# The down projection of a two-layer decoder trunk by Strassen's seven products per four blocks, with whole-block weight splitting

## The chip, the cores and the metric

The kernel runs on one core of one Trainium2 chip, as one program in one launch. The metric is the device time of one execution in microseconds (us); lower is better. TensorE (PE) multiplies; VectorE (DVE), ScalarE (ACT) and GpSimd (POOL) do the elementwise work; SyncE (SP) issues the transfers. Each engine runs its own instructions in the order in which the program gives them.

## The reference

Two layers work on one prompt of 512 tokens and 8 samples of 4 new tokens, that is 544 columns of width 1024. Only the feed-forward part is touched in its arithmetic:

```python
for l in range(DEPTH):                       # DEPTH = 2
    x = x + mixer(rms_norm(x, norm1_w[l]))   # w_in, retention and dilated attention, w_out
    x = x + conv_ffn(rms_norm(x, norm2_w[l]))
y = rms_norm(x, final_norm_w)

def conv_ffn(h, ctx, w_up_l, conv_w_l, conv_b_l, w_down_l):   # D_FF = 2816, so w_up is 1024 x 5632
    u = h @ w_up_l
    ext = jnp.concatenate([ctx, u], axis=1)
    c = conv_b_l
    for j in range(CONV_W):                  # a causal depthwise convolution of width 3
        c = c + ext[:, j:j + T] * conv_w_l[j]
    g, val = c[..., :D_FF], c[..., D_FF:]
    return (silu(g) * val) @ w_down_l        # 2816 x 1024
```

## The kernel before

**Tiles.** Activations are held with the channel on the 128 partitions and the tokens along the row. The residual stream is 8 tiles `x0` to `x7` of [128, 2, 272]: 128 channels, and the 544 tokens as two halves c of 272 columns (256 prompt and 16 sample tokens). Every large product is fp32 made of three passes in a half format: with a weight `w = wh + wl` and an activation `r = rh + rl` it is `wh·rh + wh·rl + wl·rh`. One matmul is 128x128 weights against 272 columns, and a block with k input tiles has 3 x k x 2 of them, which add up in one pair of PSUM banks called `ps` (one bank for each half of the columns).

**Weights.** Of each block SP loads a part of up to 4 input tiles into `raw` (`load_w`, six such buffers), ACT copies it into `wh` and DVE subtracts, `wl = raw - wh` (`split_w`, five pairs). A block of 8 input tiles comes in two halves.

**The feed-forward part.** There are 44 up blocks (8 input tiles, 48 matmuls each), two for each of the 22 row tiles `y` of the hidden layer: the gate and the value. What a finished bank goes through is called the conv chain below. DVE makes `u = ps * rstd` (two instructions, 512 prompt and 32 sample columns), ACT makes `c` (560 columns with the borders of the convolution), two DVE instructions add the other two taps to `c`, ACT applies SiLU for the gate, DVE multiplies the two into `y` (two instructions), ACT makes `yh` and DVE `yl`. POOL fills the borders of `u` and copies the last columns of it. The 22 tiles are taken in groups, `GROUPS`: after the up blocks of group g+1 come the 8 down blocks of group g, one for each of the 8 tiles of x, with as many input tiles as the group has (5, 5, 4, 4, 4). Each ends with one DVE instruction, `x[n] += ps` over 544 columns. The down blocks of the last group of layer 0 follow those of the group before it directly, and then `w_in` of layer 1. In layer 1 the last group goes over the columns in two passes, one for each c, so that the final norm can begin.

**Order.** PE's stream is the list `main`. All other work is written as generators of pieces, and a planner (`Stream`, with a `Clock` of its own that estimates each engine's progress) puts the pieces between PE's matmuls when it thinks that their inputs are there. Names in `URGENT` may be placed on an engine with a backlog. So the order on DVE, ACT and POOL is fixed when the program is made; on the chip an engine waits at its next instruction whatever stands behind it. All instructions pass through one helper, so they all carry line L112 (L117 after the change).

Of the kernel before, what the change touches and what calls it, by code (L numbers as in the profile page):

```python
# [9 lines left out]
F32 = mybir.dt.float32  # L10
# [14 lines left out]
GROUPS = ((0, 5), (5, 10), (10, 14), (14, 18), (18, 22))  # L25
# [17 lines left out]
EARLY = 640  # L43

# [105 lines left out]
URGENT = ("evac", "norm", "tail", "ffn", "feed", "split")  # L150
# [75 lines left out]
def trunk(ctx: ExitStack, tc: tile.TileContext, xin, w_in, w_out, w_up, w_down, kc, vc, s0, sctx_d, params_d,  # L226
# [70 lines left out]
    def add_block(src, nk, rhs, evac, pre=None):  # L297
        i = len(main)
        parts = [(0, nk)] if nk <= 4 else [(0, (nk + 1) // 2), ((nk + 1) // 2, nk)]
# [3 lines left out]

    raw, split = {}, {}

    def load_w(s):
        if s < len(halves):
            i, a, b = halves[s]
            raw[s] = rotate(wpool.tile([128, b - a, 128], F32, name=name("raw"), tag="raw", bufs=6), "raw", 6)
            sp.dma_start(raw[s], main[i]["src"][:, a:b, :])  # L310

    def split_w(s, at_once=False):
        if s < len(halves):
            i, a, b = halves[s]
# [211 lines left out]

    class Layer:
# [88 lines left out]
    def att_sample(L, l, g):  # L616
        rows = [slice(32 * i, 32 * i + 32) for i in range(4)]
        for hp in range(4):
            yield pace(L)
            kt = L.kt.pop((g, hp))  # L620
            yield PE(L.qpad, L.ks, *kt, banks=0 if hp else 2)
# [3 lines left out]
            qs = [L.qpad[:, hp, 4 * g + i, :] for i in range(4)]  # L625
# [97 lines left out]
    def ret_head(L, l, h):  # L723
# [4 lines left out]
        for b in range(NB):  # L728
            pool.tensor_mul(L.qdp[:, h, b, b * T:(b + 1) * T], q[:, SEQ + b * T:SEQ + (b + 1) * T],
# [95 lines left out]
    def ret_sample(L, l):  # L825
        yield PE(*[t for h in range(4) for t in L.s0[h]], L.qdp, L.sts, L.vss, banks=1)
        po = sec([128, 128])
        for b in range(NB):
            for h in range(4):
                pe.matmul(po[32 * h:32 * h + 32, :], lhsT=L.qdp[:, h, b, :], rhs=L.s0[h][b // 4][:, b % 4, :],  # L830
                          start=b == 0, stop=False, tile_position=(0, 32 * h))
        for h in range(4):
            pe.matmul(po[32 * h:32 * h + 32, :], lhsT=L.sts[:, h, :], rhs=L.vss[:, h, :], start=False, stop=True,
                      tile_position=(0, 32 * h))
        yield EW("dve", po)
# [22 lines left out]
    def ret_state(L, l):  # L858
        units = [(h, g) for h in range(4) for g in range(2)]
        bds = []  # L860
        for i in range(len(units) + 2):
            if i < len(units):
                h, g = units[i]
                bd = work.tile([96, 4, 128], F32R, name=name("bd"), tag="bd", bufs=3)
# [3 lines left out]
            if i >= 2:  # L868
# [7 lines left out]
                dve.scalar_tensor_tensor(s, s, DECAY_S[h], ps, op0=OP.mult, op1=OP.add)  # L876
                done()
                store(sret_o[l, h, :, g * 4:g * 4 + 4, :], s)
        L.s0 = None


    def mixer(l):
# [10 lines left out]
        def begin():  # L893
            st.spawn(norm.finish(), "norm")
            rope_tables(L, l, 2)()
            L.qpad = work.tile([128, 4, NB, 32], F32, name=name("qpad"), tag="qpad", bufs=1)
            pool.memset(L.qpad, 0.0)
            L.ks = small([128, 4, 32], "ks", 1)
            L.vs = small([32, 512], "vs", 1)
# [8 lines left out]
            def samples():  # L908
# [486 lines left out]
```

## Time and profile before

| what | value |
|---|---|
| three runs | 1446.16, 1446.17, 1448.29 us; median 1446.17 us |
| the profiled execution: its time | 1444.82 us |
| its span | 1443.0 us, mean granted TensorE clock 0.997 of full speed |
| PE busy | 1423.1 us, 99% of the span |
| DVE busy | 949.2 us, 66% |
| ACT busy | 571.6 us, 40% |
| POOL busy | 178.9 us, 12% |
| chain of work that ended last | 94% PE, 3% DVE, 1% issue |

The busy shares are means over stages with different limits. The chain of work that ended last is followed back from the last instruction; its share says on which engine the end waits.

### The profile page before, as it was taken

The numbers are of one execution on the slowest core, as the hardware profiler recorded it, in microseconds if no ns is written. First come the engines' busy times: TensorE is split into PE (matmuls) and PEld (weight loads), VectorE is DVE, ScalarE is ACT, GpSimd is POOL, SyncE is SP. The second block draws the span as 40 slices with busy tenths as digits, with TensorE's granted clock in tenths as the row PEclk, the third lists the DMA queues.
The fourth block names the chain that finished last, engine by engine and source line by source line (L and its number), as shares of the span: only waits on it lengthen the run. The fifth ranks groups of instructions, "written<-read, shape, count | busy, mean of one in ns | idle before, by whom it ended". The sixth has DMA issues, their size and how long they took to land.

```text
span 1443.0 us, 29646 instructions
## 1 busy us (share of the span) xinstructions
PE 1423.1 (99%) x11634; PEld 1356.0 (94%) x11634; DVE 949.2 (66%) x1857; ACT 571.6 (40%) x1108; POOL 178.9 (12%) x553
## 2 busy tenths in 40 slices
PE   8999999999999999999999999999999999999997
PEld 8888788999999999999998878899999999999996
DVE  8876556588775565757678765566977647566665
ACT  4454333444443333424435442243444424333334
POOL 4212222000000000000022221120000000000003
PEclk9999999999999999999999999999999999999999
DMA  6315682433222222223322339722422232322231
GB/s 237 97 60 181 233 311 89 154 113 115 93 80 88 91 83 101 93 84 104 104 90 90 119 105 316 283 91 101 148 104 88 65 112 70 107 88 89 88 93 63
DMA packets 98635, 173.92 MB, mean 121 GB/s; under 512 B 11072, under 2 KB 21440, under 8 KB 98496
## 3 DMA queue, kind: packets, MB, share of 16 engines
q1 hardware_dynamic: 98496, 172.03, 35.3%
q8 instruction: 92, 1.51, 0.4%
q14 instruction: 47, 0.39, 0.1%
HBM read 159.77 MB, written 12.21 MB: 119 GB/s over the span
## 4 chain that ended last, share of the span: by engine, by line
PE 94%; DVE 3%; issue 1%; DMA 0%; ACT 0%; SPq 0%; DVEq 0%; POOL 0%; ACTq 0%
PE ps L112 82%; PE sec L112 12%; DVE wl L112 1%; DVE rb L112 1%; DMA x<-xin 0%; DVE p L112 0%; SPq L112 0%; DVE xl L112 0%; DVE ra L112 0%; DVE sq L112 0%; ACT xh L112 0%; DVE va L112 0%; POOL qa L112 0%; DVEq L1381 0%; DVE tmp L112 0%
## 5 line engine op out<-in xcount | busy, mean ns | idle before, releaser
L112 PE MATMUL ps<-xh,wh 128*128 128x272 f32 x2304 | 489.0, 294 | 1.4 <-ACT wh L112 1.1
L112 PE MATMUL ps<-xh,wl 128*128 128x272 f32 x2304 | 477.3, 289 | 0.7 <-DVE wl L112 0.7
L112 PE MATMUL ps<-xl,wh 128*128 128x272 f32 x2304 | 477.3, 289 | 0.0
L112 PEld LDWEIGHTS ps<-xh,wh 128*128 128x128 f32 x2304 | 361.2, 189 | 19.0 <-issue 14.7
L112 PEld LDWEIGHTS ps<-xh,wl 128*128 128x128 f32 x2304 | 362.3, 189 | 0.9 <-DVE wl L112 0.9
L112 PEld LDWEIGHTS ps<-xl,wh 128*128 128x128 f32 x2304 | 362.3, 189 | 0.0
L112 ACT ACTIVATE wh<-raw 128x512 fp32r<-128x512 f32 (+2 forms) x432 | 248.3, 598 | 172.0 <-PE ps L112 158.8
L112 DVE TENSOR_TENSOR wl<-raw,wh 128x512 fp32r<-128x512 f32 (+2 forms) x432 | 295.9, 703 | 18.7 <-ACT wh L112 17.9
L112 DVE SCALAR_TENSOR_TENSOR c<-u,taps,c 128x560 f32<-128x560 f32 x176 | 141.2, 802 | 89.0 <-ACT c L112 85.9
L112 ACT ACTIVATE c<-u,taps 128x560 f32<-128x560 f32 x88 | 75.5, 857 | 227.1 <-DVE u L112 223.7
L112 DVE TENSOR_TENSOR x<-x,ps 128x544 f32<-128x544 f32 (+1 forms) x120 | 81.7, 681 | 119.6 <-PE ps L112 119.2
L112 PE MATMUL ps<-yh,wh 128*128 128x272 f32 x704 | 150.9, 288 | 0.0
L112 PE MATMUL ps<-yh,wl 128*128 128x272 f32 x704 | 150.5, 288 | 0.0
L112 PE MATMUL ps<-yl,wh 128*128 128x272 f32 x704 | 150.4, 288 | 0.0
L112 DVE TENSOR_TENSOR u<-ps,rstd 128x512 f32<-128x512 f32 (+1 forms) x176 | 69.2, 435 | 80.5 <-PE ps L112 80.4
L112 PEld LDWEIGHTS ps<-yh,wh 128*128 128x128 f32 x704 | 112.3, 188 | 0.1
L112 PEld LDWEIGHTS ps<-yl,wh 128*128 128x128 f32 x704 | 112.2, 188 | 0.1
L112 PEld LDWEIGHTS ps<-yh,wl 128*128 128x128 f32 x704 | 112.3, 188 | 0.0
L112 POOL COPY last<-u 128x2 f32<-128x2 f32 (+1 forms) x176 | 28.2, 192 | 667.2 <-DVE u L112 630.3
L112 DVE TENSOR_TENSOR rb<-ps,rope 32x544 f32<-32x544 f32 (+1 forms) x96 | 69.2, 721 | 1.4
L112 ACT ACTIVATE yh<-y 128x544 fp32r<-128x544 f32 x44 | 29.0, 659 | 82.6 <-DVE y L112 82.6
L112 PE MATMUL ps<-ch,wh 128*128 128x272 f32 x256 | 53.4, 290 | 0.0
(147 smaller groups left out, 1343.3 us busy)
## 6 DMA issues: line engine op xcount, KB each, us to landing
raw<-w_up SPq DMA_DIRECT2D x176, 256.0 KB, 2.8
raw<-w_in SPq DMA_DIRECT2D x112, 256.0 KB, 3.9
kt<-kc SPq DMA_DIRECT2D x80, 256.0 KB, 5.2
vt<-vc SPq DMA_DIRECT2D x80, 256.0 KB, 5.2
raw<-w_down SPq DMA_DIRECT2D x48, 256.0 KB, 2.6
raw<-w_out SPq DMA_DIRECT2D x32, 256.0 KB, 2.7
raw<-w_down SPq DMA_DIRECT2D x32, 192.0 KB, 2.4
s<-s SPq DMA_DIRECT2D x16, 256.0 KB, 5.3
```

What stands on the lines that cost most here:

```text
L112: return f(*args, **kw)
```

## The change

The 1024 rows of the output, in 8 tiles, and the hidden tiles of a group are taken in two by two blocks: two tiles of x (`x1` for the even, `x2` for the odd one, in the code's names), two hidden tiles a and b, each with its two column halves. What took 8 block products (2 x tiles, 2 hidden tiles, 2 halves) now takes seven, in the form that keeps partial sums (Winograd's). A *unit* is one pair of x tiles over one group: with 4 hidden tiles it has 7 products of 6 matmuls, 42 in all, where the two down blocks had 48. Strassen's form serves groups 1 to 5 of layer 0 and 1 to 4 of layer 1; group 0 and the last group of layer 1 stay plain. There are 36 units. The groups become (2, 4, 4, 4, 4, 4).

- **Weights of a unit** (`split_unit`): four raw blocks per pair of hidden tiles, in a new layout `q_down` (prepared by the host). POOL makes three sums and DVE one (256 elements per partition each, tile `sums`, one buffer; one unit at a time). ACT copies 768 elements of `raw` and 1024 of `sums` to `wh`, DVE subtracts 768 and 1024 for `wl`.
- **Activations of a pair of hidden tiles** (`make_forms`): POOL makes four differences of 272 columns (`fa`, `fb`); ACT and DVE make the hi and lo parts of them (`fh`, `fl`, 544 each, two of each) and of the plain tiles (`hb`, `lb` 544; `h1`, `l1` 272). These take the place of `yh` and `yl`.
- **Products** (`Unit`): the order on PE is P1, P7, P3 of the unit before, P6, P4, P2, P5. P1, P6, P5 and P3 add up in one bank (half 1 of `ps`), P7 and P4 in another (`sec`), P2 in half 0. Between two products that share a bank the partial sum is read: after P1 ACT copies it to `one` and POOL adds that to `x1`; after P6 and after P5 ACT copies it to `snap`, and after P5 POOL (DVE in the last group of layer 0) adds the 544 columns of `snap` to `x2`; after P7 and after P4 DVE adds 272 columns to `x2`; after P3 DVE adds 544 to `x1`. P6 waits for the copy after P1, P5 for that after P6, P3 for that after P5, P4 for DVE's addition after P7.
- **Whole blocks**: `raw`, `wh`, `wl` hold 8 input tiles in three buffers each; a block is loaded three blocks ahead and split in one instruction per engine in the middle of the block two ahead. Only the first two blocks of the program keep halves.
- **Small tiles** of the mixers (`qpad`, `qdp`, `k3`, `v3`, `vs`, `vss`, `bd`) move from pools of their own to the common buffers; two are made in two halves.

```diff
-GROUPS = ((0, 5), (5, 10), (10, 14), (14, 18), (18, 22))
+GROUPS = ((0, 2), (2, 6), (6, 10), (10, 14), (14, 18), (18, 22))
+AT = {"P1": 0, "P7": 1, "P6": 3, "P4": 4, "P2": 5, "P5": 6, "P3": 9}
+WEIGHT = {"P1": 0, "P2": 1, "P4": 2, "P5": 3, "P6": 4, "P7": 5, "P3": 6}
+UNITS = 3
...
+    def split_unit(s, nk):
+        yield IF(lambda: not splitting)
+        splitting.append(s)
+        w = raw.pop(s)
+        sums = wpool.tile([128, nk, 4, 128], F32, name=name("sums"), tag="sums", bufs=1)
...
+        yield EW("pool", w)
+        pool.tensor_add(sums[:, :, 0], w[:, :, 3], w[:, :, 2])
+        pool.tensor_sub(sums[:, :, 1], sums[:, :, 0], w[:, :, 0])
+        yield EW("act", w)
+        act.activation(hi[:, :, 0:3], w[:, :, 0:3], AF.Copy)
+        dve.tensor_sub(sums[:, :, 2], w[:, :, 0], w[:, :, 3])
+        pool.tensor_sub(sums[:, :, 3], w[:, :, 1], sums[:, :, 1])
+        yield EW("dve", hi)
+        dve.tensor_sub(lo[:, :, 0:3], w[:, :, 0:3], hi[:, :, 0:3].bitcast(F32))
+        yield EW("act", sums)
+        act.activation(hi[:, :, 3:7], sums, AF.Copy)
+        yield EW("dve", hi)
+        dve.tensor_sub(lo[:, :, 3:7], sums, hi[:, :, 3:7].bitcast(F32))
+        splitting.pop()
...
+    def make_forms(a, b, first, i, dst):
+        fa, fb = blk([128, 2, HC], F32, "fa"), blk([128, 2, HC], F32, "fb")
+        pool.tensor_sub(fa[:, 0], a[:, 1], a[:, 0])
+        pool.tensor_sub(fa[:, 1], b[:, 1], fa[:, 0])
+        pool.tensor_sub(fb[:, 0], b[:, 1], a[:, 1])
+        pool.tensor_sub(fb[:, 1], b[:, 0], fa[:, 1])
...
+    class Unit:
...
+            before = {"P4": "P7", "P6": "P1", "P5": "P6", "P3": "P5"}.get(p)
+            if before:
+                st.until(lambda: before in self.seen)
...
+            if p == "P1":
+                self.one = blk([128, HC], F32, "one")
+                act.activation(self.one, bank[:, :HC], AF.Copy)
+                yield EW("pool", self.one)
+                pool.tensor_add(x1[:, 0], x1[:, 0], self.one)
+            elif p == "P7":
+                dve.tensor_add(x2[:, 1], x2[:, 1], bank[:, :HC])
+            elif p == "P6":
+                act.activation(self.snaps[:, 0], bank[:, :HC], AF.Copy)
+            elif p == "P5":
+                act.activation(self.snaps[:, 1], bank[:, :HC], AF.Copy)
+                eng = ("dve", dve) if last else ("pool", pool)
+                yield EW(eng[0], self.snaps)
+                eng[1].tensor_add(x2, x2, self.snaps)
...
-            load_w(s + 6)
-            split_w(s + 3)
+            load_w(s + 3)
...
+                if k == (a + e) // 2:
+                    split_w(s + 2)
```

Over the whole program PE issues 216 matmuls of 272 columns fewer (24 in each of the nine groups that use the form), ACT 14 instructions fewer, DVE 30 fewer, and POOL 252 more: 108 sums, 72 differences of the forms, 36 additions of `one`, 32 of `snap` (four more are DVE's) and 4 fills of halved tiles.

The order at one place shows what stands in each engine's queue: the last up blocks before a group's down projection in the middle of layer 0, and the start of that projection (before: group 2, blocks `x0`, `x1`; after: group 3, units of `x0`, `x1` and of `x2`, `x3`). On DVE, before, the conv chain of the last up block (`u`, `c`, `y`) is followed by half-block weights and the additions from `ps`:

```order
L112 TENSOR_TENSOR wl_1312_7612<-raw_1295_7498,wh_1311_7611 128x512
L112 TENSOR_TENSOR u_1313_7640<-ps_1306_7576,rstd_829_4249 128x512
L112 TENSOR_TENSOR u_1313_7640<-ps_1306_7576,rstd_829_4249 128x8x4
L112 SCALAR_TENSOR_TENSOR c_1314_7645<-u_1313_7640,taps_78,c_1314_7645 128x560 x2
L112 TENSOR_TENSOR wl_1318_7653<-raw_1298_7530,wh_1317_7652 128x512
L112 TENSOR_TENSOR x0_69<-x0_69,ps_1315_7649 128x544
L112 TENSOR_TENSOR y_1323_7695<-c_1305_7572,c_1314_7645 128x2x256
L112 TENSOR_TENSOR y_1323_7695<-c_1305_7572,c_1314_7645 128x2x16
```

After the change, the same place on DVE:

```order
L117 TENSOR_TENSOR u_1134_7333<-ps_1129_7268,rstd_748_4092 128x512
L117 TENSOR_TENSOR u_1134_7333<-ps_1129_7268,rstd_748_4092 128x8x4
L117 TENSOR_TENSOR wl_1133_7307<-sums_1131_7305,wh_1132_7306 128x2x512
L117 SCALAR_TENSOR_TENSOR c_1135_7338<-u_1134_7333,taps_78,c_1135_7338 128x560 x2
L117 TENSOR_TENSOR x1_70<-x1_70,sec_1139_7352 128x272
L117 TENSOR_TENSOR y_1141_7375<-c_1128_7264,c_1135_7338 128x2x256
L117 TENSOR_TENSOR y_1141_7375<-c_1128_7264,c_1135_7338 128x2x16
L117 TENSOR_TENSOR sums_1142_7379<-raw_1130_7269 128x2x128
```

The weight subtraction of 1024 elements for the next unit and the two `c` instructions now stand ahead of the addition after P7 (`x1_70<-x1_70,sec`), for which P4 waits. On ACT, before and after:

```order
L112 ACTIVATE c_1314_7645<-u_1313_7640,taps_78 128x560
L112 ACTIVATE wh_1317_7652<-raw_1298_7530 128x512
L112 ACTIVATE wh_1321_7686<-raw_1307_7577 128x512
L112 ACTIVATE yh_1324_7717<-y_1323_7695 128x544
```

```order
L117 ACTIVATE c_1135_7338<-u_1134_7333,taps_78 128x560
L117 ACTIVATE one_1140_7356<-ps_1137_7344 128x272
L117 ACTIVATE snap_1138_7345<-ps_1137_7344 128x272
L117 ACTIVATE wh_1143_7380<-raw_1130_7269 128x2x384
L117 ACTIVATE wh_1143_7380<-sums_1142_7379 128x2x512
L117 ACTIVATE snap_1138_7345<-ps_1137_7344 128x272
L117 ACTIVATE one_1149_7422<-ps_1146_7407 128x272
```

The copy after P1 (`one`), for which P6 waits, stands behind the last `c` of the conv chain; the second `snap` of unit 0, for which its P3 waits, and the `one` of unit 1 stand behind the copy of 1024 `sums`, which waits for POOL. On POOL, before, only border copies stand there:

```order
L112 MEMSET u_1313_7640 128x2
L112 COPY u_1313_7640<-ctx_813_4174 128x8x2
L112 COPY last_814_4176<-u_1313_7640 128x2
L112 COPY last_814_4176<-u_1313_7640 128x16
```

After the change:

```order
L117 COPY last_733_4014<-u_1134_7333 128x16
L117 TENSOR_TENSOR x0_69<-x0_69,one_1140_7356 128x272
L117 TENSOR_TENSOR sums_1142_7379<-raw_1130_7269 128x2x128
L117 TENSOR_TENSOR sums_1142_7379<-sums_1142_7379,raw_1130_7269 128x2x128
L117 TENSOR_TENSOR sums_1142_7379<-raw_1130_7269,sums_1142_7379 128x2x128
L117 TENSOR_TENSOR x1_70<-x1_70,snap_1138_7345 128x544
L117 TENSOR_TENSOR x2_71<-x2_71,one_1149_7422 128x272
L117 TENSOR_TENSOR sums_1150_7446<-raw_1136_7342 128x2x128
L117 TENSOR_TENSOR sums_1150_7446<-sums_1150_7446,raw_1136_7342 128x2x128
L117 TENSOR_TENSOR sums_1150_7446<-raw_1136_7342,sums_1150_7446 128x2x128
```

The sums for units 2 and 3 now stand in one queue with the additions of `one` and `snap`, and every one of these instructions has its inputs in SBUF.

## Rows read from the trace of the kernel before

**Rows 1.** The page's first part: busy us, share of the span, instructions.

```profile
PE 1423.1 (99%) x11634; PEld 1356.0 (94%) x11634; DVE 949.2 (66%) x1857; ACT 571.6 (40%) x1108; POOL 178.9 (12%) x553
```

**Rows 2.** Windows of layer 0: four up blocks, then eight down blocks; busy us, clock, DMA.

```profile
576.50:600.60 24.10, 24.10 (x194) 24.10 (x193) 17.07 (x30) 10.27 (x16) 1.99 (x16) 1.00 0.29 87
600.60:624.60 24.00, 24.00 (x194) 24.00 (x193) 13.51 (x22) 6.78 (x12) 0.50 (x4) 1.00 0.28 98
```

**Rows 3.** Timeline of PE in the last stage (start us, us, operation).

```profile
1420.81 0.29 PE L112 MATMUL ps<-yh,wh 128*128 128x272 f32 x1
...
1425.20 0.29 PE L112 MATMUL ps<-yh,wl 128*128 128x272 f32 x1
1425.33 0.32 PE L112 MATMUL ps<-yh,wh 128*128 128x272 f32 x1
1425.48 0.29 PE L112 MATMUL ps<-yl,wh 128*128 128x272 f32 x1
```

**Rows 4.** Timeline of PE at the boundary from up to down blocks.

```profile
600.61 0.41 PE L112 MATMUL ps<-yh,wh 128*128 128x272 f32 x2
```

**Rows 5.** Timeline of DVE behind that boundary.

```profile
600.81 0.79 DVE L112 TENSOR_TENSOR u<-ps,rstd 128x512 f32<-128x512 f32 x2 [1.32 <-PE ps L112]
602.58 1.64 DVE L112 SCALAR_TENSOR_TENSOR c<-u,taps,c 128x560 f32<-128x560 f32 x2 [0.99 <-ACT c L112]
604.14 0.69 DVE L112 TENSOR_TENSOR wl<-raw,wh 128x512 fp32r<-128x512 f32 x1
604.74 0.72 DVE L112 TENSOR_TENSOR x<-x,ps 128x544 f32<-128x544 f32 x1
605.37 0.79 DVE L112 TENSOR_TENSOR y<-c,c 128x512 f32<-128x512 f32 x2
```

**Rows 6.** Timeline of ACT there.

```profile
601.69 0.86 ACT L112 ACTIVATE c<-u,taps 128x560 f32<-128x560 f32 x1 [2.70 <-DVE u L112]
```

**Rows 7.** Groups of DVE by shape, whole span: busy us, mean ns, idle before.

```profile
L112 DVE TENSOR_TENSOR wl<-raw,wh 128x512 fp32r<-128x512 f32 x368 | 267.2, 740 | 18.7 <-ACT wh L112 17.9
L112 DVE TENSOR_TENSOR wl<-raw,wh 128x256 fp32r<-128x256 f32 x32 | 13.4, 419 | 0.0
L112 DVE TENSOR_TENSOR x<-x,ps 128x272 f32<-128x272 f32 x16 | 6.9, 433 | 5.8 <-PE ps L112 5.8
```

**Rows 8.** Groups of ACT by shape.

```profile
L112 ACT ACTIVATE wh<-raw 128x512 fp32r<-128x512 f32 x368 | 220.5, 621 | 127.6 <-PE ps L112 118.3 <-issue 6.8 <-DMA raw<-w_down 1.2
L112 ACT ACTIVATE wh<-raw 128x256 fp32r<-128x256 f32 x32 | 13.1, 411 | 27.6 <-PE ps L112 27.6
L112 ACT ACTIVATE sq<-x 128x272 f32<-128x272 f32 x16 | 6.9, 432 | 19.3 <-DVE x L112 19.0
```

**Rows 9.** Groups of POOL by shape.

```profile
L112 POOL TENSOR_TENSOR qd<-qr,cst 128x512 f32<-128x512 f32 x8 | 10.2, 1278 | 0.0
L112 POOL TENSOR_TENSOR sq<-sq,sq 128x272 f32<-128x272 f32 x5 | 3.9, 773 | 29.8 <-ACT sq L112 29.8
```

**Rows 10.** Timeline of DVE in the first microseconds, while POOL works too.

```profile
12.96 1.58 DVE L112 TENSOR_TENSOR wl<-raw,wh 128x512 fp32r<-128x512 f32 x1
14.46 1.89 DVE L112 SCALAR_TENSOR_TENSOR xl<-x,par,xh 128x544 fp32r<-128x544 f32 x1
16.27 0.68 DVE L112 TENSOR_TENSOR wl<-raw,wh 128x512 fp32r<-128x512 f32 x1
```

**Rows 11.** Timeline of POOL there.

```profile
12.41 1.57 POOL L112 TENSOR_TENSOR sq<-x 128x544 f32<-128x544 f32 x1
14.06 1.70 POOL L112 TENSOR_TENSOR sq<-sq,sq 128x544 f32<-128x544 f32 x1
15.70 0.96 POOL L112 MEMSET qpad<- 128x1024 f32 x1
```

**Rows 12.** Timeline of DVE in the last stage.

```profile
1424.78 0.42 DVE L112 TENSOR_TENSOR x<-x,ps 128x272 f32<-128x272 f32 x1
```

**Rows 13.** Timeline of POOL in the last stage.

```profile
1423.18 5.94 POOL L112 TENSOR_TENSOR yo<-yo,rstd 128x544 f32<-128x544 f32 x4 [6.25 <-DVE rstd L112]
```

**Rows 14.** DMA issues: KB each, median us from issue to landing.

```profile
raw<-w_up SPq DMA_DIRECT2D x176, 256.0 KB, 2.8
```

More of the change, by code (lines that the diff above doesn't have):

```diff
@@ L149 @@
 SHARE = 1.0
-URGENT = ("evac", "norm", "tail", "ffn", "feed", "split")
+URGENT = ("evac", "norm", "tail", "ffn", "feed", "split", "snap")
 class Stream:
@@ L302, in add_block, with add_units @@
             halves.append((i, a, b))
+    def add_units(src, k0, nk, forms, evac, pre=None, end=None):
+        main.append(dict(units=MP, nk=nk, forms=forms, evac=evac, pre=pre, end=end, first=len(halves)))
+        for m in range(MP):
+            halves.append((len(main) - 1, src[m, :, k0:k0 + nk], nk))
     raw, split = {}, {}
+    splitting = []
+    def split_unit(s, nk):
[3 more added lines that the diff above has]
+        sums = wpool.tile([128, nk, 4, 128], F32, name=name("sums"), tag="sums", bufs=1)
+        hi, lo = (rotate(wpool.tile([128, nk, 7, 128], F32R, name=name(n), tag=n, bufs=UNITS), n, UNITS)
+                  for n in ("wh", "wl"))
+        yield EW("pool", w)
[12 more added lines that the diff above has]
+        splitting.pop()
+        split[s] = (hi, lo)
     def load_w(s):
@@ L825, in ret_sample @@
     def ret_sample(L, l):
-        yield PE(*[t for h in range(4) for t in L.s0[h]], L.qdp, L.sts, L.vss, banks=1)
+        yield PE(*[t for h in range(4) for t in L.s0[h]], *L.qdp, L.sts, L.vss, banks=1)
         po = sec([128, 128])
@@ L895, in begin @@
             rope_tables(L, l, 2)()
-            L.qpad = work.tile([128, 4, NB, 32], F32, name=name("qpad"), tag="qpad", bufs=1)
-            pool.memset(L.qpad, 0.0)
+            L.qpad = [blk([128, 2, NB, 32], F32, "qpad") for _ in range(2)]
+            for t in L.qpad:
+                pool.memset(t, 0.0)
             L.ks = small([128, 4, 32], "ks", 1)
-            L.vs = small([32, 512], "vs", 1)
+            L.vs = blk([32, 512], F32, "vs")
             L.os = small([128, 4, NB, T], "os", 1)
@@ L1110, in conv @@
             dve.tensor_mul(y[:, :, PC:HC].rearrange("p c (b t) -> p c b t", t=T), tail(g), tail(c))
+            if j == FB - 1:
+                for s in range(2):
+                    store(conv_o[l, :, s * FB:(s + 1) * FB], F.last[s])
+                norm.parts = {}
+                F.ready = len(GROUPS)
+            if any(j in range(*GROUPS[gi]) for gi in strassen):
+                F.raw[j] = y
+                return
             yield EW("act", y)
@@ L1117, in conv @@
             F.y[j] = (h, lo)
-            if j == FB - 1:
-                for s in range(2):
-                    store(conv_o[l, :, s * FB:(s + 1) * FB], F.last[s])
-                norm.parts = {}
         def up(s, j):
@@ L1182, in trunk @@
     load_w(4)
-    load_w(5)
     for what, n in start:
@@ new lines, in trunk, with run_later, run_units @@
+    later = []
+    def run_later():
+        unit, p, end = later.pop()
+        unit.step(p)
+        end()
+    def run_units(b):
+        units = [Unit(b, m, b["first"] + m) for m in range(b["units"])]
+        steps = sorted((7 * m + at, m, p) for m in range(b["units"]) for p, at in AT.items())
+        for at, m, p in steps:
+            if later and at == 3:
+                run_later()
+            if at < 7 * b["units"]:
+                units[m].step(p)
+            else:
+                later.append((units[m], p, b["end"]))
@@ L1233, in trunk @@
             b["pre"]()
+        if "units" in b:
+            run_units(b)
+            continue
         ps = main_bank()
@@ L1257, in trunk @@
             for k in range(nk):
+                if later and k == 2:
+                    run_later()
                 r = b["rhs"](k)
```

162 lines of the change are left out of this document (131 added, 31 removed).

## The prediction

> **What bounds the kernel now.** I read the page's shares first: PE is busy for 99% of the span [rows 1], so the kernel ends when PE has issued its matmuls, and time goes away only with matmuls. Second, what one matmul costs: in the last stage 35 starts take 1425.20 - 1420.81 = 4.39 us, 0.1254 us each [rows 3]. Third, how the stages stand: four up blocks fill PE for 24.10 of 24.1 us and leave DVE 7.0 us of slack, eight down blocks fill it for 24.00 of 24.0 us and leave DVE 10.5 us; POOL has 0.5 us of work there [rows 2]. So nothing stalls PE now, DVE has room, and POOL is empty. Fourth, the boundary from up to down blocks, since there the conv chain of the last up block still runs while the down blocks begin: I take its times from the timelines of PE, DVE and ACT [rows 4 to 6]. PE rolls over it because an `x += ps` has a second pair of banks to be late in.
>
> **What goes.** 216 matmuls at 0.1254 us: **-27.1 us**, 3.0 us in each of the nine groups. PE is the bound, so all of it would show if nothing stalled.
>
> **What comes, and why POOL decides.** Before, a bank was read once, when complete. Now a unit's partial sums are read in the middle, by an engine that has other work in front of the read, and PE stands until it is done. The second new thing is 252 instructions on POOL, and the trace shows what POOL does to DVE. At 12.96 a `wl` of 512 elements took 1.58 us and the next instruction 1.89, while POOL's 1.57 and 1.70 us lay beside them; the first `wl` after POOL had gone on to a memset took 0.68 [rows 10, 11]. The ends of the two engines alternate: what is seen is one working while the other stands. An addition that reads PSUM took 0.42 us under POOL's `yo` [rows 12, 13], the price that the same shape has in the mean [rows 7]. So I count POOL's additions and DVE's instructions with two SBUF inputs as one queue, and those that read PSUM apart.
>
> The Trainium skill, "SBUF — State Buffer", section "Who interferes with whom", says the same as a rule: VectorE with two SBUF inputs and GpSimd reading SBUF take one shared pair of ports exclusively, and the later one blocks for the other's whole instruction. It speaks against this change, and the trace agrees, 0.68 against 1.58 us. Without it the sum below would be that of the first rival.
>
> **Prices.** POOL: half of `qd` (512 elements, 1.28 us) is 0.64, so 0.65 for a sum of 256 elements, 0.7 for 272 (773 ns is the nearest row), 1.3 for 544 [rows 9]. DVE: `wl` of 256 takes 0.42, of 512 undisturbed 0.69, so 0.96 for 768 and 1.23 for 1024; neighbours overlap by 0.09 (the `wl` at 604.14 is followed after 0.60), which leaves 0.33, 0.87 and 1.14 [rows 5, 7]. ACT: 411 and 621 ns for 256 and 512, so 1.04 for 1024, and 0.43 for 272 columns [rows 8].
>
> **An ordinary group** (seven: 8 up blocks, then 4 units). I count from its first matmul, 600.61 in the row [rows 4]. P6's turn comes after 12 matmuls, at 1.50. It waits for ACT's `one`, which stands behind the last `c`. That starts at 601.69 and takes 0.86 [rows 6], so it ends at 1.94; with 0.43 for `one` P6 starts at about 2.4: **0.9 late**. P4's turn is then at 3.15. It waits for DVE's addition after P7. DVE is through `u` at 0.99, then has `wl` of 1024 (to 2.13), the two `c` of 1.64 together (to 3.77), then the addition, 0.43 with a small overlap, to 4.1 [rows 5, 7]: **1.0 late**. That is 1.9 us a group even if POOL disturbs nobody: the lower bound. Nothing waits here in the kernel before, because the same `c` is followed by additions that may be late.
>
> With the queue shared, POOL's `x += one` (0.7) gets between the `c` instructions and in front of the P7 addition: 2.6 us. While units 0 and 1 run, the weights of units 2 and 3 are split. That takes POOL 3 x 0.65, its two additions 0.7 + 1.3, together 3.95, and DVE 0.33 + 0.87 + 1.14 = 2.34: 6.3 us of one queue against 42 x 0.1254 = 5.27 us of PE, 1.0 us more in each. Behind the last sum stand ACT's copy and the next `one` or `snap`, so PE sees it. Upper bound 2.6 + 2.0 = 4.6. I take 3.3, the middle: the first of the two microseconds lies largely under unit 0's own waits, and the up blocks give the queue time to catch up. **7 x 3.3 = +23.1 us** (13.3 to 32.2).
>
> **The last two groups of layer 0** run back to back, eight units without up blocks between. In their first five units (210 matmuls, 26.3 us) the order has on POOL 18 sums, 8 differences of the last group's forms, 6 additions of `one` and 4 of `snap`: 11.7 + 5.6 + 4.2 + 5.2 = 26.7 us, as much as PE. DVE has five splits (5 x 2.34 = 11.7), the forms' lo parts (six of 544 at about 0.63, two of 272 at 0.38: 4.6) and the end of the conv chain and an addition (1.8), 18.1 us with SBUF inputs. One queue of 44.8 us against 26.3: 18.5 late. Lower bound 4 (1.9 at the start as above, 2 more for the forms, since POOL alone has no slack); upper 22, with the last three units, in which DVE has about 17 us of work against 15.5 of PE and the norm waits for it. I take **+17 us**, close to the upper bound, since every product of a unit hangs on this queue and nothing else can be put in front. PE has no other work to take up there: what follows is `w_in`, which needs the finished x.
>
> **The groups of 2 tiles** (two). Their eight down blocks are 12 matmuls, 12.0 us together, half of the eight down blocks in [rows 2]. DVE has in them eight additions at 0.63 (5.0) and about 8.6 of weights and conv chain: 13.6, so 1.6 too much. An up block is now 512 KB in one transfer, issued three blocks ahead, 4.5 us; 256 KB take 2.8 us [rows 14], so it needs between 2.8 and 5.6, and may be 1.1 late. Bounds 1.0 and 4.0; I take 2.5: **+5 us**.
>
> **At nothing.** Whole-block splitting: two `wl` of 512 at 0.60 against one at 1.14 gives DVE 0.06 a block back, the same order on ACT; DVE's 7 us of slack per four up blocks [rows 2] hides it either way, and loads that come later are hidden too where a block takes 6 us. If that cover failed it would cost some 2 us. The moved small tiles, the halved fills: POOL's fills at the mixers' start, off the path. 252 products begin in a bank of their own or again in one: at such a place the last stage shows 0.15 instead of 0.125 [rows 3], 0.025 x 252 = 6.3 us at most; I take 0, as inside `ps` no bank is opened anew, and keep it for the upper end.
>
> **The sum.** -27.1 + 23.1 + 17 + 5 = +18.0. Against the profiled execution of 1444.82 us that is 1462.8; the median of the runs shown lies 1.35 above that execution, so **1464 us**.
>
> **The rivals.** *Faster, the shared queue doesn't bite.* Everything stands at the lower bounds: 7 x 1.9 + 4 + 2 x 1.0 = 19.3, so -7.8: 1438 us. For it: most of POOL's new instructions could fall where DVE reads PSUM or stands (7 and 10.5 us idle in the two windows [rows 2]). Against it: rows 10 and 11, and that POOL alone equals PE in the last two groups. It decides at 27.1 us of stalls in all: with the last two groups at 17 and the short ones at 5, an ordinary group would have to lose under 0.75, which the copy behind `c` alone exceeds; with ordinary groups at 1.9 the last two would have to lose under 9. *No change.* The queue bites only where units follow without up blocks, and half as much: 13.3 + 10 + 4 = 27.3, so 1446 us. *Worse.* Also the sums for units 0 and 1, made under the last two up blocks, push `c` and `y` back, and the bounds are reached everywhere: 32.2 + 22 + 8 + 6.3 = 68.5, so +41: 1488 us. Against it: in an ordinary period the shared queue has some 58 us of 69 of PE (DVE's 37 with SBUF inputs, POOL's 21, counted at the prices above), so it catches up.
>
> **How the numbers follow.** Forecast 0.55, faster 0.24, no change 0.08, worse 0.13. The forecast's own range is 1450 to 1475. To leave out no more than 2 in 10 the range goes down to 1437, into the faster case, and up to 1484, into the worse: 1437 to 1484. A change of 0.2%, 2.9 us, is what a measurement can tell: faster by more 0.23 (nearly all of the first rival), within 0.08, slower 0.69.
>
> **What would show it.** In the profile after: PE idle before P6 with ACT as releaser and before P4 with DVE (after the first matmuls of each group, 0.9 and 1.0 us); `wl` of 768 and 1024 and `c` longer than here where POOL adds, POOL's share up by some 190 us; the last two groups of layer 0 taking about 59 us for 336 matmuls (42.1). Wrong it would be if POOL's additions take well under 0.65 us, if the two `c` keep their 1.64 us beside them, if PE is still 99% busy, or if PE waits for weights or transfers that I count as hidden.

## The result, and the profile after

The changed kernel takes 1500.99 us (median of 4 runs, 1499.58 to 1503.17) against 1446.38 us: 1.038 times the time before, 95% interval 1.0366 to 1.0390. It is slower by 54.6 us where 18 were forecast. Its span is 1499.1 us, 56.1 longer. The page's first part, answering to [rows 1]:

```profile
PE 1428.6 (95%) x11418; PEld 1343.6 (90%) x11418; DVE 1067.6 (71%) x1827; ACT 629.1 (42%) x1094; POOL 484.4 (32%) x805
```

PE has 216 matmuls fewer and still more busy time; POOL has 305 us more, not 190. Windows by stage show where the time went (length, then busy us and count of PE, its weight loads, DVE, ACT, POOL; granted clock, DMA). In order: first mixer up to `w_out`, down blocks of the group of 2 tiles, the 8 up blocks behind them, an ordinary group up to the next up block, the last two groups of layer 0, second mixer:

```profile
5.49:276.52 271.03, 263.25 (x2166) 227.02 (x2165) 171.42 (x379) 103.67 (x232) 64.20 (x98) 0.99 0.49 169
402.39:419.15 16.76, 13.07 (x99) 12.28 (x97) 13.70 (x25) 7.72 (x14) 3.98 (x8) 1.00 0.35 119
419.15:468.81 49.66, 49.66 (x384) 49.66 (x385) 32.09 (x47) 16.60 (x21) 11.27 (x34) 0.97 0.30 96
542.68:567.46 24.78, 21.25 (x165) 20.52 (x164) 19.77 (x27) 11.21 (x19) 16.57 (x15) 1.00 0.25 86
690.03:756.10 66.07, 48.18 (x332) 44.47 (x331) 55.81 (x71) 34.93 (x60) 46.77 (x42) 0.96 0.23 76
756.10:1021.74 265.64, 260.49 (x2172) 225.50 (x2171) 160.67 (x372) 97.07 (x222) 54.61 (x90) 1.00 0.44 152
```

The same mixers before, from their first `w_in` matmul to the first of `w_out`:

```profile
5.55:270.40 264.85, 258.72 (x2166) 226.41 (x2165) 179.60 (x406) 106.95 (x259) 65.14 (x96) 0.99 0.51 177
720.75:978.71 257.96, 255.05 (x2166) 223.62 (x2165) 166.55 (x395) 98.92 (x246) 55.88 (x89) 1.00 0.46 160
```

I call *loss* the length of a stretch less its matmuls at 0.1254 us [rows 3]; I count the matmuls that start in it, while the windows also count those that reach over an edge. The ordinary group has 162 up to the next up block: 24.78 - 20.3 = 4.5 us; all seven lose 4.5 to 4.8, together 32.4. The last two groups have 330 there: 66.07 - 41.4 = 24.7, 25.5 with the start of the next stretch. The short blocks lose 16.76 - 12.0 = 4.7, the up blocks behind them 1.5 more; 12.4 in both layers. The mixers are longer by 6.2 and 6.1 (in the second 0.75 of units' matmuls and 0.8 of the last groups' loss are taken off). The last stage loses 1.1 more, which no run was made for. 32.4 + 25.5 + 12.4 + 12.3 + 1.1 - 27.1 = 56.6, against 56.1 measured.

The boundary of [rows 4 to 6] after the change, from the group that starts at 542.68 (timeline of all engines):

```profile
543.38 0.78 DVE L117 TENSOR_TENSOR u<-ps,rstd 128x512 f32<-128x512 f32 x2
544.08 1.21 DVE L117 TENSOR_TENSOR wl<-sums,wh 128x1024 fp32r<-128x1024 f32 x1
544.26 0.85 ACT L117 ACTIVATE c<-u,taps 128x560 f32<-128x560 f32 x1 [0.69 <-DVE u L117]
545.02 0.38 ACT L117 ACTIVATE one<-ps 128x272 f32<-128x272 f32 x1
545.21 2.17 DVE L117 SCALAR_TENSOR_TENSOR c<-u,taps,c 128x560 f32<-128x560 f32 x2
545.45 0.39 PE L117 MATMUL ps<-fh,wh 128*128 128x272 f32 x1 [1.10 <-ACT one L117]
546.02 0.76 POOL L117 TENSOR_TENSOR x<-x,one 128x272 f32<-128x272 f32 x1
547.30 0.42 DVE L117 TENSOR_TENSOR x<-x,sec 128x272 f32<-128x272 f32 x1
547.78 0.39 PE L117 MATMUL sec<-fh,wh 128*128 128x272 f32 x1 [1.32 <-DVE x L117]
557.55 1.06 ACT L117 ACTIVATE wh<-sums 128x1024 fp32r<-128x1024 f32 x1 [1.53 <-POOL sums L117]
558.51 0.38 ACT L117 ACTIVATE one<-ps 128x272 f32<-128x272 f32 x1
558.95 0.39 PE L117 MATMUL ps<-fh,wh 128*128 128x272 f32 x1 [1.11 <-ACT one L117]
```

P6 waits for `one` behind `c`, P4 for the addition behind the two `c`, which take 2.17 instead of 1.64 with POOL's addition beside them: the first two waits are where the prediction put them. With the slow start behind each they cost 1.4 and 1.6 us. A third of 1.4 us follows at P6 of unit 2: its `one` stands behind the copy of the sums, which waits for POOL. Three of the seven groups look like this. In the other four PE spends some 14 matmuls behind the second wait at half its clock, about 1.5 us (last section), and the third wait is gone but for 0.2 us in one of them. By shape, whole span (mean ns of one in the middle):

```profile
L117 DVE TENSOR_TENSOR wl<-raw,wh 128x768 fp32r<-128x768 f32 x36 | 41.3, 1148 | 4.2 <-ACT wh L117 4.2
L117 DVE TENSOR_TENSOR lb<-y,hb 128x544 fp32r<-128x544 f32 x18 | 23.5, 1306 | 9.1 <-ACT hb L117 9.1
L117 DVE TENSOR_TENSOR x<-x,ps 128x544 f32<-128x544 f32 x84 | 60.0, 715 | 27.7 <-PE ps L117 27.7
L117 POOL TENSOR_TENSOR sums<-sums,raw 128x256 f32<-128x256 f32 x36 | 39.8, 1107 | 2.8
L117 POOL TENSOR_TENSOR x<-x,one 128x272 f32<-128x272 f32 x36 | 38.4, 1068 | 12.9 <-ACT one L117 12.6
```

### The profile page after: what moved, and what is told of

It reads as the page before. It is cut to its first block, busy times and chain, and to the rows that moved or that the text cites. A ratio compares the mean times of both kernels' runs of the same rounds, so it can differ in the third digit from the quotient of the medians.

```text
span 1499.1 us, 28716 instructions
## 1 busy us (share of the span) xinstructions
PE 1428.6 (95%) x11418; PEld 1343.6 (90%) x11418; DVE 1067.6 (71%) x1827; ACT 629.1 (42%) x1094; POOL 484.4 (32%) x805
## 4 chain that ended last, share of the span: by engine, by line
PE 72%; DVE 15%; POOL 5%; issue 3%; ACT 3%; DMA 1%; SPq 0%; DVEq 0%; ACTq 0%; POOLq 0%
PE ps L117 59%; PE sec L117 13%; DVE c L117 3%; DVE wl L117 3%; DVE p L117 3%; DVE rb L117 2%; POOL sums L117 2%; POOL x L117 1%; DVE u L117 1%; ACT wh L117 1%; DVE x L117 1%; DVE y L117 1%; DVE ra L117 1%; DMA raw<-w_up 1%; DMA vt<-vc 1%
## 5 line engine op out<-in xcount | busy, mean ns | idle before, releaser
L117 PEld LDWEIGHTS ps<-xh,wh 128*128 128x128 f32 x2304 | 363.0, 190 | 25.5 <-issue 15.5
L117 DVE TENSOR_TENSOR wl<-raw,wh 128x1024 fp32r<-128x1024 f32 (+3 forms) x238 | 258.8, 1089 | 23.1 <-ACT wh L117 22.7
L117 ACT ACTIVATE wh<-raw 128x1024 fp32r<-128x1024 f32 (+3 forms) x238 | 212.9, 895 | 86.7 <-PE ps L117 65.4
L117 POOL COPY last<-u 128x2 f32<-128x2 f32 (+1 forms) x176 | 62.6, 387 | 377.9 <-DVE u L117 377.9
L117 DVE TENSOR_TENSOR x<-x,ps 128x544 f32<-128x544 f32 (+1 forms) x100 | 66.9, 670 | 33.1 <-PE ps L117 33.1
L117 DVE CUSTOM_DVE_ANT_0 p<-sec,cst 128x128 f32<-128x128 f32 (+3 forms) x64 | 29.2, 488 | 53.0 <-PE sec L117 52.8
L117 POOL TENSOR_TENSOR x<-x,snap 128x544 f32<-128x544 f32 x32 | 47.0, 1468 | 53.3 <-ACT snap L117 52.4
L117 ACT ACTIVATE wh<-sums 128x1024 fp32r<-128x1024 f32 x36 | 38.2, 1060 | 53.4 <-POOL sums L117 29.6
L117 PE MATMUL ps<-fh,wh 128*128 128x272 f32 x144 | 44.0, 305 | 17.1 <-ACT one L117 17.1
L117 ACT ACTIVATE snap<-ps 128x272 f32<-128x272 f32 x72 | 28.2, 392 | 66.7 <-PE ps L117 66.7
L117 PE MATMUL sec<-fh,wh 128*128 128x272 f32 x144 | 44.0, 305 | 12.5 <-DVE x L117 12.5
```

Of the source, the lines that this page charges most:

```text
L117: return f(*args, **kw)
```

## The experiments

Losses below are read as above; "before" in each comparison is between 1445.9 and 1447.0 us.

### Does POOL hold DVE up? Fills instead of additions, and everything on DVE

```diff
+    def fill(dst, *ins):
+        pool.charge("tensor_add", [dst], list(ins), (), {})
+        for _ in range(2):
+            nc.gpsimd.memset(dst, 1.0)
...
-        pool.tensor_add(sums[:, :, 0], w[:, :, 3], w[:, :, 2])
+        fill(sums[:, :, 0], w[:, :, 3], w[:, :, 2])
...
```

> The changed kernel, in the same order on every engine, but each of POOL's 248 new additions is replaced by two fills of its destination with a constant (the sums, differences and additions to x are left out; a fill of 1024 elements takes 0.96 us, so two fills of 256 or 544 should take about as long as the addition did). POOL then has the same load but reads no SBUF. Theory (POOL's additions and DVE's instructions with two SBUF inputs shut each other out): the wl and c instructions fall back to their lengths without POOL, an ordinary group loses 2 to 2.5 us to waits instead of 4.6, the last two groups of layer 0 lose 4 to 8 instead of 25.5, and the time is 1455 to 1475 us. Rival (the waits come from the order alone: who stands ahead of whom): within 6 us of the changed kernel's 1501.

Measured: 1468.01 us. The two rows of DVE that were longest, and the group and the last two groups as windows:

```profile
L117 DVE TENSOR_TENSOR wl<-raw,wh 128x768 fp32r<-128x768 f32 x36 | 34.4, 955 | 8.3 <-ACT wh L117 8.2
L117 DVE TENSOR_TENSOR lb<-y,hb 128x544 fp32r<-128x544 f32 x18 | 13.0, 720 | 9.1 <-ACT hb L117 9.1
```

```profile
539.45:562.00 22.55, 21.16 (x165) 20.58 (x164) 16.68 (x27) 10.50 (x19) 11.33 (x29) 1.00 0.28 94
682.08:735.30 53.22, 46.22 (x333) 43.57 (x331) 43.82 (x71) 33.90 (x60) 27.02 (x80) 0.97 0.29 94
```

The lengths fall back to 955 and 720 ns (952 and 719 in the next run, where POOL adds nothing). POOL still works beside DVE: the fills take it 167 us, where the additions would take 187 at the prediction's prices and took 269 beside DVE. But the fills only write SBUF, and DVE's lengths are undisturbed: it is POOL's reading of SBUF that shuts DVE out. An ordinary group loses 2.2 us; its two waits at unit 0 cost 0.9 and 1.0, the prediction's figures for a POOL that disturbs nobody. The last two groups lose 11.8, more than the 4 to 8 expected. The exclusion is worth up to 33 us of the 55 (up to, since the fills wait for no inputs either). But with it gone the kernel is still 22 us slower than before.

The next run puts the additions on DVE:

```diff
-        yield EW("pool", w)
-        pool.tensor_add(sums[:, :, 0], w[:, :, 3], w[:, :, 2])
+        yield EW("dve", w)
+        dve.tensor_add(sums[:, :, 0], w[:, :, 3], w[:, :, 2])
...
```

> The changed kernel with POOL's 248 new additions issued on DVE instead, nothing left out. Theory of the shared queue: the one queue stays but gets shorter, since DVE takes 0.33 to 0.65 us where POOL takes 0.65 to 1.4; ordinary groups lose about 3 us, the last two groups of layer 0 some 15, time 1480 to 1490. Rival (no exclusion, POOL and DVE work side by side): some 100 us of work move onto the engine that PE waits for, and the time rises above 1505.

Measured: 1507.63 us, as the rival had it, though not for its reason: the lengths are undisturbed here too. An ordinary group loses 6.2 to 8.0 us. PE's row shows where: P4's wait for the addition after P7 is 20.3 us in all where the changed kernel has 12.5. A read of PSUM, which POOL never held up, now stands behind the sums in one queue. The total length of the queue, by which I had counted, says too little; what matters is what stands ahead of the reads.

```profile
L117 PE MATMUL sec<-fh,wh 128*128 128x272 f32 x144 | 47.1, 327 | 20.4 <-DVE x L117 20.3
```

### The mixers

```diff
-            L.qpad = work.tile([128, 4, NB, 32], F32, name=name("qpad"), tag="qpad", bufs=1)
+            L.qpad = [blk([128, 2, NB, 32], F32, "qpad") for _ in range(2)]
...
-                bd = work.tile([96, 4, 128], F32R, name=name("bd"), tag="bd", bufs=3)
+                bd = blk([96, 4, 128], F32R, "bd")
...
```

> The kernel before with only one part of the change: the mixers' small tiles in the common buffers. In the changed kernel each mixer is 6.2 us longer than before, and SP there waits for buffers that DVE, POOL and PE free, ahead of the loads of the cached values. Theory (eight of 51 common buffers held by small tiles, loads come late): 1455 to 1460 us. Rival (the mixers lose their time to the whole-block loads and splits): 1446 to 1448.

Measured: 1454.01 us, 1.0055 (1.0040 to 1.0070). Its mixers take 6.5 and 4.2 us more than before:

```profile
5.77:277.12 271.35, 264.47 (x2164) 228.81 (x2165) 180.09 (x406) 107.14 (x259) 65.67 (x98) 0.98 0.51 172
727.65:989.85 262.20, 258.19 (x2167) 224.12 (x2165) 166.57 (x395) 99.09 (x246) 55.76 (x90) 1.00 0.47 157
```

Then the same with room for 60 common buffers:

```diff
-NBLK = 51
+NBLK = 60
```

> The kernel before with the mixers' small tiles in the common buffers, and with 60 of these buffers instead of 51 (the small tiles' own pools are gone, so there is room). Theory (the small tiles take buffers away, and loads and elementwise tiles wait for one to come free): back to the kernel before, 1445 to 1448 us. Rival (not the number but the sharing: a tile that lives long stands in the way when its turn comes, or the halved fills): 1452 to 1455, as with 51.

Measured: 1446.40 us, 1.0007 (0.9998 to 1.0016), no longer to be told from before. So it is the number of buffers; 1.6 of the 12.3 us by which the changed kernel's mixers are longer stay without a run. In the changed kernel the cost shows as waits of SP, which issues the loads of the cached values `vt` (what SP's queue waited for at 905 to 932, then what waits for `vt`):

```profile
SPq L117 <- PE sec L117: 5.1, 5, 3.6
SPq L117 <- DVE rb L117: 4.7, 1, 4.7
SPq L117 <- POOL kr L117: 1.7, 1, 1.7
```

```profile
who waited for it (us, times):
  POOL qr L117: 5.3, 1
  PEld sec L117: 4.8, 7
```

SP stands until a buffer's last readers are through, the load lands late, and PE's weight loads wait 4.8 us for it. SP waits in the kernel before, too, but at the same place PE's weight loads wait only 1.0 us for `vt`.

### The short group

> The kernel before with only the groups of the change (2, 4, 4, 4, 4, 4), all plain. In the changed kernel the two groups of 2 tiles and the two up blocks behind them lose 6 us each. Theory (eight additions of 544 from PSUM, the weights and the conv chain in 12 us of PE are too much for DVE): 2 to 5 us a group, 1450 to 1456. Rival (the 512 KB loads, issued only three blocks ahead, come late, and the short group itself is harmless): 1446 to 1448.

Its edit is the line `GROUPS` alone, all plain. Measured: 1445.63 us, 0.9999 (0.9990 to 1.0009), the rival: the short group alone loses 1.1 us in each layer, which the comparison can't tell from nothing. Then the changed kernel without it:

```diff
-GROUPS = ((0, 2), (2, 6), (6, 10), (10, 14), (14, 18), (18, 22))
+GROUPS = ((0, 6), (6, 10), (10, 14), (14, 18), (18, 22))
```

> The changed kernel with a plain first group of 6 tiles instead of a plain one of 2 and a Strassen one of 4: 48 matmuls more (6.0 us), two ordinary groups fewer (9.3 us of waits), and no blocks of 1.5 us. Theory (loads and splits of 8 tiles, three and two blocks ahead, come too late where blocks are short, which costs 2 x 6 us): 1484 to 1488 us. Rival (those 6 us belong to the forms and the first unit and come back behind the longer group): 1493 to 1498.

Measured: 1486.24 us, as the theory had it. In the changed kernel's timeline the load of an up block is issued at 412.11, and PE starts the block at 419.15:

```profile
412.11 6.61 SPq L117 DMA_DIRECT2D raw<-w_up  x4
416.05 1.06 ACT L117 ACTIVATE wh<-raw 128x1024 fp32r<-128x1024 f32 x1 [3.64 <-DMA raw<-w_up]
417.14 1.23 DVE L117 TENSOR_TENSOR wl<-raw,wh 128x1024 fp32r<-128x1024 f32 x1 [1.86 <-ACT wh L117]
418.29 0.71 DVE L117 TENSOR_TENSOR x<-x,ps 128x544 f32<-128x544 f32 x1
419.15 0.49 PE L117 MATMUL ps<-xh,wh 128*128 128x272 f32 x2 [2.60 <-DVE x L117]
```

The transfer takes 3.9 us, then come two whole-block instructions one after the other, and the addition that frees the bank is queued behind the second. In the run with the groups alone a part has at most 4 input tiles and is loaded six parts ahead, here six short blocks instead of three: the load of the same up block is issued at 396.52 and PE starts it at 411.21, 14.7 us later instead of 7.0. The other losses of the short blocks are two waits of 0.7 and 0.4 us for their `wl`; the 1.5 us behind are PE at half its clock (last section). No run changed the loads alone, so their share is read from the trace.

### The last two groups of layer 0

```diff
-        strassen = range(1, len(GROUPS) - (l == DEPTH - 1))
+        strassen = range(1, len(GROUPS) - 1)
```

> The changed kernel with the last group of layer 0 plain (24 matmuls more, 3.0 us). Theory (eight units in a row without up blocks between are more than POOL and DVE can serve): the stretch of the last two groups loses 5 to 8 us instead of 25.5, time 1483 to 1488. Rival (most of the loss lies at the end of the layer, where the norm waits for the last additions): above 1496.

Measured: 1485.46 us. With four units and then plain blocks this stretch of 360 matmuls loses 6.1 us instead of 25.5:

```profile
691.87:743.09 51.22, 48.33 (x363) 47.87 (x362) 39.19 (x55) 26.98 (x44) 18.01 (x21) 0.93 0.30 88
```

In the changed kernel's timeline PE's waits are spread over all of the stretch, 16 of them from 692.80 to 753.72. So the loss belongs to units in a row, not to the end of the layer.

### What an ordinary group waits for

```diff
-AT = {"P1": 0, "P7": 1, "P6": 3, "P4": 4, "P2": 5, "P5": 6, "P3": 9}
+AT = {"P1": 0, "P7": 1, "P2": 3, "P6": 4, "P4": 5, "P5": 6, "P3": 9}
```

> The changed kernel with one number table changed: P2, which adds to nothing, comes before P6 instead of after P4, so that P6 and P4 have 0.75 us more before they need the copy of P1 and the addition of P7, and P5 has 0.75 us less after P6. Theory (what an ordinary group loses is the distance between a partial sum and its read at unit 0, 0.9 and 1.0 us, once each): about 1.0 to 1.5 us less a group, 1488 to 1494 us. Rival (the work of POOL and DVE in the units is too long, so that a wait saved in one place comes back at P5 and P3): within 4 us of 1501.

Measured: 1503.16 us. PE's row: P2 itself waits.

```profile
L117 PE MATMUL ps<-hb,wh 128*128 128x272 f32 x144 | 44.6, 310 | 20.4 <-ACT one L117 17.1 <-ACT snap L117 3.3
```

17.1 us is what P6 waited for `one` in the changed kernel. P2 adds to nothing, but it writes the other half of the tile that ACT reads, and the program's wait is for the whole tile (the run that gives P2 a bank of its own, below, bears this out). So this run doesn't test the distance. The next one does:

```diff
+                if k == a + HOIST and "units" in main[i + 3] and "units" not in b:
+                    hoist(main[i + 3])
...
```

> The changed kernel with P1 and P7 of a group's first unit moved into the last up block before it (ahead of its sixth input tile, 2.25 us of matmuls before its end), wherever an up block stands before units (eight places). ACT's copy of P1 and DVE's addition of P7 then stand ahead of that block's u and c instead of behind them. Theory (2.2 to 2.8 us of what a group loses are the two waits behind the last conv chain): an ordinary group loses 1.5 to 2.5 us instead of 4.6, time 1480 to 1486 us. Rival (POOL and DVE are behind anyway, and the waits come back at the next product that needs them): 1494 us or more.

Measured: 1503.02 us, the rival. The two waits at unit 0 are gone, and the group loses 4.5 us as before, at other places. On ACT:

```profile
545.49 0.37 ACT L118 ACTIVATE snap<-ps 128x272 f32<-128x272 f32 x1
545.76 0.83 ACT L118 ACTIVATE wh<-raw 128x768 fp32r<-128x768 f32 x1
549.24 1.06 ACT L118 ACTIVATE wh<-sums 128x1024 fp32r<-128x1024 f32 x1 [2.65 <-POOL sums L118]
550.21 0.38 ACT L118 ACTIVATE snap<-ps 128x272 f32<-128x272 f32 x1
```

ACT stands 2.65 us at the copy of the sums, and the `snap` that P3 needs stands behind it; PE's matmul at 550.64 waits 1.44 for it. What was won in front is waited for here. Two more runs took the causes together and the order on ACT:

> The kernel with P1 and P7 moved ahead, in which POOL's additions are replaced by fills as in the first run of fills (the sums, differences and additions to x are left out). Each alone left an ordinary group 4.6 (moved) and 2.2 us (fills) of waits. Theory (two causes, either of which hides the other: unit 0's products come right behind the conv chain, and the shared queue is late by about as much): together under 0.5 us a group, time 1448 to 1456 us. Rival (a third cause, such as one unit being split at a time, holds the group): 2 us a group as with the fills alone, 1464 us or more.

Measured: 1467.34 us, the rival; 1.9 us a group. The two causes don't add up to the whole: a third was left.

```diff
-            cost = 0.1 + n * (2.2 if len(ins) > 1 else 1.0) / 1000
+            cost = 0.1 + n * (3.8 if len(ins) > 1 else 1.0) / 1000
```

> The kernel with P1 and P7 moved ahead, and the planner told what POOL's additions take in the trace (1.07 us for 256 elements instead of 0.66; one number in its cost). It then puts ACT's snap and one ahead of the copy of the sums that waits for POOL. Theory (with the moved products the waits come from that place in ACT's queue): an ordinary group loses 2 to 3 us, 1485 to 1492 us. Rival (the length of the shared queue decides, and the waits move on to the weights): 1498 us or more.

Measured: 1495.90 us, between theory and rival; 4.0 to 4.4 us a group. The place on ACT was worth half a microsecond at most; unit 0's P2 now waited 1.1 us for the `snap` of P6. So P2 got a bank of its own:

```diff
+            elif p == "P2":
+                st.until(lambda: st.banks > 0)
+                self.z2 = sec([128, 512])
...
-                dve.tensor_add(x1, x1, self.ps[:, :, :HC])
+                dve.tensor_add(x1[:, 1], x1[:, 1], bank[:, :HC])
```

> The same with POOL's real additions: P1 and P7 moved ahead, the planner's cost of POOL raised, P2 in a bank of its own. Theory (shared tile): 4.05 us of waits in an ordinary group fall to 2 to 2.5, time 1480 to 1486 us. Rival (the shared queue's length decides): 1492 us or more.

Measured: 1483.02 us; 2.4 to 2.5 us a group instead of 4.0, the theory's numbers. The group, with 150 matmuls behind the two products moved ahead:

```profile
542.37:563.61 21.24, 19.53 (x152) 18.87 (x151) 18.00 (x29) 10.09 (x17) 15.80 (x15) 1.00 0.30 100
```

With fills instead of additions:

> P1 and P7 moved ahead, POOL's additions replaced by fills (sums, differences and additions to x left out), and P2 in a bank tile of its own, which DVE adds to x with 272 columns. Until now P2 waits for ACT's snap of P6, though it adds to nothing: it writes the other half of the same ps tile. Theory (that shared tile holds the last 2 us of an ordinary group and some of the last two groups): under 0.7 us a group, 1448 to 1456 us. Rival (the wait moves on to P5 and P3, which need the snaps in any case): 1462 us or more.

Measured: 1461.17 us, a miss; 1.6 us a group (under 0.7 expected), 8.6 in the last two groups. What is left in a group are short waits of P4 for the addition after P7 and of P3 for its `snap`, in the last two groups mostly P5's three waits for its `snap` (1.9, 1.6 and 1.0 us).

### Taking the losses away together

> The last kernel with a plain first group of 6 tiles and a plain last group in layer 0 too, so that Strassen's form is left in six groups (144 matmuls fewer than before, 18.0 us). Theory (the four losses add up and can be taken away one by one; the mixers' 12 us stay, since there is no room for more common buffers): 1452 to 1458 us, still slower than before. Rival (they depend on each other, what is saved at one place is waited for at the next): 1464 to 1470.

Measured: 1470.39 us, 0.4 above the rival's range; the six groups still lost 4.5 us or more each. With P2's own bank and the raised cost:

> The same three edits on the version with a plain first group of 6 tiles and a plain last group in layer 0 (1470 us, 144 matmuls fewer than before). Theory (shared tile): 2 us less in each of six groups, 1455 to 1461 us, which is still above the kernel before, since the mixers' 12 us stay. Rival: 1466 us or more.

Measured: 1451.87 us, 1.0036 (1.0025 to 1.0046), better than expected. Then memory: part of a unit's weights goes into common buffers, and there are 57 of these.

```diff
-NBLK = 51
+NBLK = 57
...
+        ha, la = (blk([128, nk, 2, 128], F32R, n) for n in ("ha", "la"))
-        hi, lo = (rotate(wpool.tile([128, nk, 7, 128], F32R, name=name(n), tag=n, bufs=UNITS), n, UNITS)
+        hi, lo = (rotate(wpool.tile([128, nk, 5, 128], F32R, name=name(n), tag=n, bufs=UNITS), n, UNITS)
```

> The version of 1452 us with memory moved: the hi and lo weights of P1 and P2 (512 elements) go into common buffers, which leaves 5 KB instead of 7 in each of the six weight buffers and room for 57 common buffers instead of 51. Theory (the mixers' loss of 6 to 7 us in layer 0 and 3 in layer 1 comes from too few common buffers): 1443 to 1447 us. Rival (the units now take common buffers themselves, or the two smaller copies and subtractions per unit cost as much): 1450 us or more.

Measured: 1447.01 us, 1.0003 (0.9994 to 1.0011): as fast as before. Its mixers take 267.00 and 256.45 us, against 264.85 and 257.96:

```profile
5.76:272.76 267.00, 259.75 (x2165) 227.64 (x2165) 169.19 (x379) 103.55 (x232) 63.08 (x98) 0.99 0.49 172
724.57:981.02 256.45, 254.74 (x2166) 224.03 (x2165) 155.49 (x368) 95.32 (x219) 52.22 (x90) 1.00 0.47 159
```

The groups pay 0.4 to 0.6 us more each (2.9 to 3.7 instead of 2.5 to 3.1), which I put down to the two extra copies and subtractions.

The next run is the version of 1452 us with P6 moved ahead, too:

```diff
-HOIST = 5
+HOIST = {4: "P1", 5: "P7", 7: "P6"}
...
```

> The version of 1452 us with P1, P7 and P6 of a group's first unit moved ahead instead of P1 and P7 (ahead of the fifth, sixth and eighth input tile of the last up block). Theory (ACT's snap of P6 stands behind the last c, which costs 0.5 us a group): 1447 to 1450 us. Rival (the wait of 1.4 us at the third unit, behind the copy of the sums, takes it back): 1451 to 1453.

Measured: 1453.00 us, the rival: 2.7 to 3.0 us a group.

> Both edits together. Theory (they touch different stages and add): 1438 to 1444 us, below the kernel before. Rival: 1446 us or more.

Measured: 1448.23 us, 1.0011 (1.0002 to 1.0019), the rival. No version with units came out below the kernel before.

## Why the prediction was right in its direction and wrong in its size

Of the 38.6 us by which the losses exceed the prediction's sum, 12.3 lie in the mixers, 9.3 in the ordinary groups, 8.5 in the last two groups of layer 0, 7.4 in the groups of 2 tiles and 1.1 in the last stage. Its last sign of being wrong came true: PE waits for weights and transfers that it counted as hidden.

- **"What goes", -27.1 us:** right; away from the waits a matmul still costs 0.125 us in the units (66 starts in 8.29 us behind 548.64), so the 6.3 us kept for banks opened again did not come.
- **The shared queue of POOL and DVE:** shown by the fills, and the largest cost, up to 33 us. The rule that the prediction quotes from the Trainium skill ("SBUF — State Buffer", section "Who interferes with whom") agrees with this case's trace: 1148 against 955 ns, 1306 against 720, and the additions that read PSUM unchanged (719 and 715).
- **"An ordinary group", 3.3:** it was 4.6, the upper bound. The step that failed in its size is "the first of the two microseconds lies largely under unit 0's own waits". It doesn't: unit 0's waits cost 2.9 where 2.6 were counted, and behind them come 1.4 at unit 2, or as much at half the clock, where 0.7 were. And a wait taken away comes back at the next product, as the run with P1 and P7 moved ahead shows. One wait I hadn't seen, P2's for a read of the other half of its tile, is worth 1.5 us of a group once the others are gone.
- **"The last two groups of layer 0", 17:** 25.5, above the upper bound of 22. The mechanism held, since four units before plain blocks lose 6.1. The step that failed is the lower bound of 4: with the exclusion gone the stretch loses 11.8, in waits for the snaps, copies and additions in a row, and still 8.6 where P1 and P7 are moved ahead and P2 has its own bank. Beyond the start and the forms I had counted nothing for them.
- **"The groups of 2 tiles", 5:** 12.4. The load "may be 1.1 late" left out what stands between landing and PE: two whole-block instructions in a row and an addition behind the second. PE waits 2.6 to 2.7 us for them in each layer, and half its clock behind them costs some 1.5 more.
- **"At nothing", the moved small tiles, 0:** 12.3. This is the step that was wrong in kind. I priced the instructions and not the buffers: held tiles push back every load that takes a buffer of the same set. With them alone the mixers were 6.5 and 4.2 us longer, and with 60 buffers nothing was left of it.
- **The rivals.** "The shared queue doesn't bite", 1438, is the run with fills: 1468. Of the 30 us between, 12.6 are the mixers, 7.8 the short groups and 7.8 the last two groups; the ordinary groups stood nearly where it had them, at 2.0 to 2.2 against 1.9. "Worse" (1488) came nearest, still 13 us below.

## What to carry to other kernels

A product that is read in the middle of its sum puts three in-order queues behind every matmul; count what stands ahead of each read on its engine, not the length of the queues, and expect a wait taken away to come back at the next read. Work that looks free on an idle GpSimd isn't, while VectorE has two SBUF inputs to read. A tile moved into common buffers costs what waits for a buffer, on the queue that issues the loads.

## What the runs showed of the hardware that was not expected

At the end of a wait, or within a microsecond behind it, PE's clock may fall to half for some 3 us, so that a wait can be paid twice. Windows of the changed kernel: a wait, the stretch behind it, the rest of the up blocks, and a stretch within the last two groups:

```profile
416.30:419.10 2.80, 0.24 (x2) 0.02 (x1) 1.96 (x3) 2.43 (x3) 0.00 (x0) 1.00 0.44 176
420.10:423.10 3.00, 3.00 (x15) 3.00 (x15) 1.80 (x3) 0.00 (x0) 0.00 (x0) 0.50 0.83 270
423.50:468.80 45.30, 45.30 (x364) 45.30 (x363) 29.34 (x44) 16.14 (x20) 11.27 (x34) 1.00 0.26 83
727.20:730.40 3.20, 3.20 (x16) 3.20 (x16) 2.10 (x5) 1.13 (x2) 3.04 (x4) 0.50 0.28 113
```

At 0.50, that is 1.2 GHz, a matmul of 272 columns starts every 0.227 us instead of 0.125. Behind the first mixer there are eight such stretches of 13 to 15 matmuls in the changed kernel, 114 in all, and none in the one before: about 11 us at 0.1 each, contained in the losses above. Where the clock fell inside an ordinary group, the group lost hardly more than the others (4.6 to 4.8 with such a stretch, 4.5 to 4.7 without): the third wait was gone or shorter by as much. How much of the 11 us would be won by keeping the clock up was not tried.
